# Modulation groups 9 to 14: the matmuls of two weight units issued as a pair, the later unit first

## The chip, the cores and the metric

The kernel runs on one core of a Trainium2 chip. PE is the matmul engine (its weight loads are shown apart as PEld), DVE the vector engine, ACT the scalar engine; SP issues nearly all transfers from HBM. The metric is the device time of one execution in microseconds. The kernel before took 1195.18 us, the median of 3 runs (1194.2 to 1197.44).

## The reference

One layer of a decoder trunk on 256 tokens of width 2048, all in float32:

```python
mod = jax.nn.silu(c) @ w_ada[l] + b_ada[l]          # 2048 -> 6 x 2048, one vector per sequence
shift_m, scale_m, gate_m, shift_f, scale_f, gate_f = jnp.split(mod[:, None, :], 6, axis=-1)
h = rms_norm(x, norm_mix_g[l]) * (1.0 + scale_m) + shift_m
proj = h @ w_in[l]                                   # q, k, v | xs, z, B, C, dt
...                                                  # attention on 8 heads; SSD (Mamba-2) on 16 heads
mix = jnp.concatenate([attn, ssm], axis=-1) @ w_out[l]
x = x + gate_m * mix
h = rms_norm(x, norm_ffn_g[l]) * (1.0 + scale_f) + shift_f
x = x + gate_f * conv_ffn(h, w_up[l], conv_ffn_w[l], conv_ffn_b[l], w_down[l])
```

`mod`, the modulation, is a product of one vector with a 2048 x 12288 matrix of 100 MB. `MOBA_BLOCK` is 256, the length of the sequence, so attention is plain causal attention with a bias.

## The kernel before, in words

Activations are kept transposed (features on partitions, 256 tokens along the row). Each weight matrix comes in units of 128 x 2048 float32 (1 MB). A gemm unit is split after landing: ACT casts it to a rounded high part (line 258), DVE subtracts to get the low part (line 259), and PE does three matmuls for each 128 x 128 block (lines 277 to 279), 48 for a unit.

The modulation's 96 columns of 128 are 24 groups of four, and each group comes as four units. For most groups DVE multiplies a unit with the broadcast vector and sums (line 210). For the groups in `ON_PE` (0, 6, 9 to 14 and 16) PE does it: unit i of a group holds a quarter of the rows for all four column blocks, and its four matmuls (line 217, tile `adp`, k = 0 to 3) each take a 128 x 32 stationary piece of the silu of c and stream 512 columns of the unit. Matmul k writes the partitions 32k to 32k+31 of one PSUM tile, so the four write different quarters of it, and the four units of a group add up there. After the last unit ACT copies the tile out (`row`, line 221) and four matmuls of one column turn it into columns (line 224, tile `adc`).

The order of the work is set in two steps. The table `ORDER` gives the program order up to the FFN: tokens such as `ada.9.0` (group 9, unit 0), V, Q, B, Z (input projection), S0 to S2 (attention of one head), T1 and T2 (SSD of two heads), O (output projection). Then a scheduler deals the instructions out to each engine's list by priority, which is the program order unless it is raised: the steps in `HPS`, attention and SSD among them, run under `tc.high_priority(offset=HP)`. Each engine works through its list in order; waits are semaphores. In the names of the lists, `wa` is the input projection's accumulator, `oa` the output projection's, `s`, `bp`, `pt`, `o` belong to attention, `xt` (line 533) is a transpose for SSD, `sg` and `y` (lines 577 and 578, four matmuls for two heads, on 64-column halves) are SSD's matmuls, `u1a` is the first FFN accumulator.

Weight units and modulation units share buffers: from the token `open` (before group 8) to `close2` (after group 14 has begun) there are three, `ws`; behind `close2` six. A buffer goes to the next transfer when its last reader is done, for a gemm unit DVE's second subtraction, for a modulation unit on PE its last matmul. SP issues the transfers in order and waits for that.

Of the kernel before, what the change touches and what calls it, by code (L numbers as in the profile page):

```python
# [30 lines left out]
HP = 200  # L31
# [63 lines left out]
def hymba_layer(ctx, tc, xT, c_row, cT, w_ada, vecs, consts, relb, onehot, w_vdt, w_in, w_out, w_up1, w_up, w_dn, outT):  # L95
    nc = tc.nc
    dve, act, pool, pe = nc.vector, nc.scalar, nc.gpsimd, nc.tensor
# [33 lines left out]
    def aux_tile(name):  # L131
        return psp.tile([P, 512], F32, tag="aux", name=name, bufs=7 - NACC)

    def tmp(name, n=T, tag="t256", bufs=4, dt=F32):
        return tp.tile([P, n], dt, tag=tag, name=name, bufs=bufs)
# [10 lines left out]
    c32 = cp.tile([P, KT, 32], F32, name="c32")  # L146
# [47 lines left out]
        return vec[:, CV[name] + i:CV[name] + i + n]  # L194


    ada_ps = {}

    def ada_load(g, i):
        ws = ws_tile(f"ada{g}_{i}")  # L200
        nc.sync.dma_start(ws[:, :D], w_ada[4 * g + i])
        return ws
# [3 lines left out]
    def ada_unit(g, i):  # L206
        ws = ada_pre.pop((g, i)) if (g, i) in ada_pre else ada_load(g, i)
        if g not in ON_PE:
            j = GROUPS[g][i]
            dve.scalar_tensor_tensor(ws[:, :D], ws[:, :D], 1.0, cb, op0=ALU.mult, op1=ALU.mult,  # L210
                                     accum_out=mod[:, j:j + 1])
            return
        if i == 0:
            ada_ps[g] = psp.tile([P, 512], F32, tag="ada", name=f"adp{g}", bufs=1)
        ps = ada_ps[g]
        for k in range(4):
            pe.matmul(ps[32 * k:32 * k + 32, :], c32[:, 4 * i + k, :], ws[:, k * 512:(k + 1) * 512],
                      start=i == 0, stop=i == 3)
        if i == 3:
            row = tmp(f"row{g}", 512, "row", 1)  # L220
            act.copy(row, ps)
            pc = aux_tile(f"adc{g}")
            for k in range(4):
                pe.matmul(pc[:, k:k + 1], row[:, k * P:(k + 1) * P], ones[:, 0:1], start=True, stop=True)
            t = GROUPS[g]
            if t[0] + 1 == t[1]:
                dve.tensor_copy(mod[:, t[0]:t[0] + 4], pc[:, 0:4])
            else:
                dve.tensor_copy(mod[:, t[0]:t[0] + 2], pc[:, 0:4:2])
                dve.tensor_copy(mod[:, t[1]:t[1] + 2], pc[:, 1:4:2])  # L230
# [9 lines left out]
    def ada_some(n, last=24):  # L240
        for _ in range(n):
            g, i = ada_next[0]
            if g < last:
                ada_unit(g, i)
                ada_next[0] = [g, i + 1] if i < 3 else [g + 1, 0]
# [19 lines left out]
    def weight_unit(src, n, name, hw=1024):  # L265
        ws = get_unit(src, n, name)
        parts = [hi_lo_part(ws, o, min(hw, n - o), name) for o in range(0, n, hw)]

        def block(i):
            wh, wl = parts[i * P // hw]  # L270
            j = i * P % hw
            return wh[:, j:j + P], wl[:, j:j + P]

        return parts, block
# [393 lines left out]
    def ada_step(g, i):  # L668
        ada_unit(g, i)
        if g < 8:  # L670
            if g in ON_PE:
                if i == 3:
                    ada_params(0, 2 * g, 2, "g_mix")
            elif i % 2:
                ada_params(0, 2 * g + i // 2, 1, "g_mix")
        else:
            ada_next[0] = [g, i + 1] if i < 3 else [g + 1, 0]
# [16 lines left out]
    for i in range(6):  # L694
        pe.matmul(ss1[:, 0:T], ones, (sqs[:, 1, i * T:i * T + T] if i < 4 else sqs[:, 0, (i - 4) * T:(i - 3) * T]),
                  start=i == 0, stop=i == 5)
# [27 lines left out]
    gp = mkpool("gT", NHALF + GX)  # L724
    h2 = fp.tile([P, KT, 512], F32R, name="h2")
    ada_unit(16, 0)
    rs2 = stats()

# [59 lines left out]
    for half in range(2):  # L788
        gts = []
        for jj in range(NHALF):  # L790
            j = half * NHALF + jj
            if half == 0:
                w = weight_unit(w_up1[NHALF + j], 2048, f"u2_{j}")
# [15 lines left out]
        for i in range(KT):  # L809
# [5 lines left out]
            for q in range(2):  # L815
                w = weight_unit(w_dn[half, i, q], 11 * P, f"d{half}_{i}_{q}")
# [106 lines left out]
```

## Time and profile before

| | |
|---|---|
| median of 3 runs | 1195.18 us (1194.2 to 1197.44) |
| profiled execution | 1199.98 us, span 1198.2 us |
| PE busy | 1166.6 us, 97% |
| DVE busy | 913.4 us, 76% |
| ACT busy | 636.7 us, 53% |
| granted clock, mean | 0.988 of 2.4 GHz |
| read from HBM | 305.98 MB, 257 GB/s over the span |

The profile is one execution. Busy time counts each engine's instructions; PE's are pipelined and overlap, so what one of them costs is better read from the distance between starts. A line of the profile is a line of the kernel before. The modulation groups 9 to 14 run between 243 and 424 us, and the FFN begins at 459 us.

### The profile page before, as it was taken

The numbers are of one execution on the slowest core, as the hardware profiler recorded it, in microseconds if no ns is written. First come the engines' busy times: TensorE is split into PE (matmuls) and PEld (weight loads), VectorE is DVE, ScalarE is ACT, GpSimd is POOL, SyncE is SP. The second block draws the span as 40 slices with busy tenths as digits, with TensorE's granted clock in tenths as the row PEclk, the third lists the DMA queues.
The fourth block names the chain that finished last, engine by engine and source line by source line (L and its number), as shares of the span: only waits on it lengthen the run. The fifth ranks groups of instructions, "written<-read, shape, count | busy, mean of one in ns | idle before, by whom it ended". The sixth has DMA issues, their size and how long they took to land.

```text
span 1198.2 us, 23400 instructions
## 1 busy us (share of the span) xinstructions
PE 1166.6 (97%) x9760; PEld 1115.8 (93%) x9760; DVE 913.4 (76%) x1371; ACT 636.7 (53%) x959; POOL 0.9 (0%) x7
## 2 busy tenths in 40 slices
PE   7899999999999999999999999999999999999996
PEld 4899999988888898999999999999999999999995
DVE  3899969977988898776599974446888889666554
ACT  4545434357786545445567654444555555555552
POOL 0000000000000000000000000000000000000000
PEclk8899999999999999999999999999999999999998
DMA  9989898777766996986565545557888776545552
GB/s 367 409 305 361 321 344 308 263 266 266 280 234 227 368 383 254 353 320 226 185 204 184 200 147 194 194 194 276 295 299 309 283 264 231 187 153 197 195 194 96
DMA packets 47443, 309.59 MB, mean 258 GB/s; under 512 B 5568, under 2 KB 6761, under 8 KB 16105
## 3 DMA queue, kind: packets, MB, share of 16 engines
q1 hardware_dynamic: 46170, 307.04, 70.2%
q10 hardware_dynamic: 1168, 1.06, 0.4%
q8 instruction: 76, 1.25, 0.4%
q14 instruction: 29, 0.24, 0.1%
HBM read 305.98 MB, written 2.11 MB: 257 GB/s over the span
## 4 chain that ended last, share of the span: by engine, by line
PE 85%; DVE 6%; DMA 5%; ACT 2%; issue 1%; SPq 0%; DVEq 0%; ACTq 0%
PE da L279 7%; PE da L278 7%; PE da L277 7%; PE ua L279 6%; PE ua L277 6%; PE ua L278 6%; PE wa L277 5%; PE wa L279 4%; PE wa L278 4%; PE va L348 4%; PE u2a L278 3%; PE u2a L277 3%; PE u2a L279 3%; PE oa L277 2%; PE oa L279 2%; PE oa L278 2%
## 5 line engine op out<-in xcount | busy, mean ns | idle before, releaser
L258 ACT CAST h_u<-s_u 128x1024 fp32r<-128x1024 f32 x176 | 183.4, 1050 | 187.0 <-PE ua L278 88.6
L259 DVE TENSOR_TENSOR l_u<-s_u,h_u 128x1024 fp32r<-128x1024 f32 x176 | 213.1, 1222 | 67.7 <-ACT h_u L258 67.3
L279 PE MATMUL ua<-h,l_u 128*128 128x256 f32 x704 | 194.4, 276 | 1.3 <-DVE l_u L259 1.3
L278 PE MATMUL ua<-h,h_u 128*128 128x256 f32 x704 | 194.3, 276 | 0.0
L277 PE MATMUL ua<-h,h_u 128*128 128x256 f32 x704 | 194.3, 276 | 0.0
L278 PE MATMUL da<-g,h_d 128*128 128x256 f32 x704 | 194.3, 276 | 0.0
L279 PE MATMUL da<-g,l_d 128*128 128x256 f32 x704 | 194.3, 276 | 0.0
L277 PE MATMUL da<-g,h_d 128*128 128x256 f32 x704 | 194.1, 276 | 0.0
L259 DVE TENSOR_TENSOR l_d<-s_d,h_d 128x1024 fp32r<-128x1024 f32 (+1 forms) x128 | 108.8, 887 | 83.6 <-ACT h_d L258 83.6
L277 PE MATMUL wa<-hT,h_w 128*128 128x256 f32 x576 | 163.9, 285 | 4.7 <-ACT h_w L258 3.7
L278 PE MATMUL wa<-hT,h_w 128*128 128x256 f32 x576 | 161.0, 280 | 0.0
L279 PE MATMUL wa<-hT,l_w 128*128 128x256 f32 x576 | 160.3, 281 | 0.2 <-DVE l_w L259 0.2
L258 ACT CAST h_d<-s_d 128x1024 fp32r<-128x1024 f32 (+1 forms) x128 | 98.2, 782 | 115.0 <-PE da L278 106.8
L210 DVE SCALAR_TENSOR_TENSOR ada<-ada,cb 128x2048 f32<-128x2048 f32 x60 | 136.9, 2285 | 16.1 <-DMA ada<-w_ada 16.0
L279 PEld LDWEIGHTS ua<-h,l_u 128*128 128x128 f32 x704 | 132.2, 188 | 1.5 <-DVE l_u L259 1.5
L278 PEld LDWEIGHTS da<-g,h_d 128*128 128x128 f32 x704 | 132.2, 188 | 0.0
L278 PEld LDWEIGHTS ua<-h,h_u 128*128 128x128 f32 x704 | 132.2, 188 | 0.0
L279 PEld LDWEIGHTS da<-g,l_d 128*128 128x128 f32 x704 | 132.2, 188 | 0.0
L277 PEld LDWEIGHTS ua<-h,h_u 128*128 128x128 f32 x704 | 132.2, 188 | 0.0
L277 PEld LDWEIGHTS da<-g,h_d 128*128 128x128 f32 x704 | 132.1, 188 | 0.0
L258 ACT CAST h_w<-s_w 128x1024 fp32r<-128x1024 f32 x72 | 73.7, 1048 | 90.4 <-PE wa L278 45.6
L277 PEld LDWEIGHTS wa<-hT,h_w 128*128 128x128 f32 x576 | 109.5, 190 | 13.0 <-ACT h_w L258 5.8
(237 smaller groups left out, 2681.9 us busy)
## 6 DMA issues: line engine op xcount, KB each, us to landing
ada<-w_ada SPq DMA_DIRECT2D x96, 1024.0 KB, 6.7
s_u<-w_up SPq DMA_DIRECT2D x88, 1024.0 KB, 4.9
s_d<-w_dn SPq DMA_DIRECT2D x64, 704.0 KB, 4.1
s_w<-w_in SPq DMA_DIRECT2D x36, 1024.0 KB, 6.9
s_o<-w_out SPq DMA_DIRECT2D x16, 1024.0 KB, 6.7
s_v<-w_vdt SPq DMA_DIRECT2D x8, 1040.0 KB, 7.9
x<-xT SPq DMA_DIRECT2D x4, 512.0 KB, 4.6
outT<-x SPq DMA_DIRECT2D x2, 640.0 KB, 3.0
```

What stands on the lines that cost most here:

```text
L210: dve.scalar_tensor_tensor(ws[:, :D], ws[:, :D], 1.0, cb, op0=ALU.mult, op1=ALU.mult, accum_out=mod[:, j:j + 1])
L258: act.copy(wh[:, :m], ws[:, o:o + m])
L259: dve.tensor_sub(wl[:, :m], ws[:, o:o + m], wh[:, :m].bitcast(F32))
L277: pe.matmul(o, whs, a[:, 0:T], start=first, stop=False)
L278: pe.matmul(o, whs, a[:, T:2 * T], start=False, stop=False)
L279: pe.matmul(o, wls, a[:, 0:T], start=False, stop=last)
L348: pe.matmul(va[tt][i][:, :n], lo if st == 1 else hi, (wl if st == 2 else wh)[:, s], start=f and st == 0, stop=l and st == 2)
```

## The change

For the groups 9 to 14 (`8 <= g < 16`; those of them that are on PE) the first of two units is only loaded and kept. When the second is there, its four matmuls are issued, at raised priority, and tied behind them the four of the first. The start flag of the group's accumulation moves to unit 1, the stop flag to unit 2. Groups 0, 6 and 16 go the old way.

```diff
-    ada_ps = {}
+    ada_ps, ada_held = {}, {}
...
         ps = ada_ps[g]
-        for k in range(4):
-            pe.matmul(ps[32 * k:32 * k + 32, :], c32[:, 4 * i + k, :], ws[:, k * 512:(k + 1) * 512],
-                      start=i == 0, stop=i == 3)
+
+        def products(n, w, first, last):
+            for k in range(4):
+                m = pe.matmul(ps[32 * k:32 * k + 32, :], c32[:, 4 * n + k, :], w[:, k * 512:(k + 1) * 512],
+                              start=first, stop=last)
+            return m
+
+        if 8 <= g < 16:
+            if i % 2 == 0:
+                ada_held[g] = ws
+                return
+            with tc.high_priority(offset=HP):
+                m = products(i, ws, i == 1, False)
+                with tc.issue_after(m.ins):
+                    products(i - 1, ada_held.pop(g), False, i == 3)
+        else:
+            products(i, ws, i == 0, i == 3)
         if i == 3:
```

The scheduler deals out a new order from there. PE's list is the same up to the 1662nd matmul, at 243 us, and again from a little behind the head of the FFN. SP's list differs in two places only (one unit of the output projection and one of group 16, each by a place or two). Lines of the changed kernel are 14 higher from line 218 on; the products are on its line 219.

PE's list in the middle of the input projection's last quarter, before: unit 3 of group 9 alone, between gemm matmuls and the second matmul stage of an attention head (`o`).

```order
L277 MATMUL wa_12_2840<-hT_142,h_w_2810 128x256
L278 MATMUL wa_12_2840<-hT_142,h_w_2810 128x256
L279 MATMUL wa_12_2840<-hT_142,l_w_2811 128x256
L217 MATMUL adp_2642<-ada_3_2899,c_98 32x512 x4
L467 MATMUL o_2888<-pts_2886,vdt 128x256
L468 MATMUL o_2888<-pts_2886,vdt 128x128
```

The same unit now, with unit 2 behind it, among the transposes (`pt`) of another head:

```order
L456 MATMUL s_2862<-qk_146 128x128
L219 MATMUL adp_2642<-ada_3_2895,c_98 32x512
L476 MATMUL pt_2878<-con,p_2730 128x128
L219 MATMUL adp_2642<-ada_3_2895,c_98 32x512
L477 MATMUL pt_2878<-con,p_2730 128x128
L219 MATMUL adp_2642<-ada_3_2895,c_98 32x512 x2
L219 MATMUL adp_2642<-ada_2_2798,c_98 32x512 x4
L292 MATMUL wa_12_2810<-hT_141,h_w_2802 128x256
```

Unit 3 has moved 36 matmuls forward, unit 2 32 matmuls back; the four matmuls of unit 3 stand in three pieces.

PE's list at the SSD output of the first two heads (`y`, T2.0), in the output projection's first half, before:

```order
L577 MATMUL y_3770<-L_3656,xdt 64x256
L578 MATMUL y_3770<-L_3656,xdt 64x128
L577 MATMUL y_3770<-L_3656,xdt 64x256
L578 MATMUL y_3770<-L_3656,xdt 64x128
L277 MATMUL oa_1_3852<-cat_3093,h_o_1_3848 128x256
L278 MATMUL oa_1_3852<-cat_3093,h_o_1_3848 128x256
L279 MATMUL oa_1_3852<-cat_3093,l_o_1_3849 128x256
L277 MATMUL oa_1_3852<-cat_3248,h_o_1_3848 128x256
L278 MATMUL oa_1_3852<-cat_3248,h_o_1_3848 128x256
L533 MATMUL xt_3776<-con,cxs 128x128 x2
```

And now:

```order
L293 MATMUL oa_1_3852<-cat_3024,l_o_1_3849 128x256
L591 MATMUL y_3766<-L_3652,xdt 64x256
L547 MATMUL xt_3772<-con,cxs 128x128
L592 MATMUL y_3766<-L_3652,xdt 64x128
L547 MATMUL xt_3772<-con,cxs 128x128
L591 MATMUL y_3766<-L_3652,xdt 64x256
L592 MATMUL y_3766<-L_3652,xdt 64x128
L571 MATMUL sg_2_3785<-am,tri_r 128x512
```

The four matmuls of `y`, in one piece before, stand in three pieces with a transpose in each gap.

## Rows read from the trace of the kernel before

**Rows 1.** The page: busy us (share of the span) and instructions of each engine.
```profile
PE 1166.6 (97%) x9760; PEld 1115.8 (93%) x9760; DVE 913.4 (76%) x1371; ACT 636.7 (53%) x959; POOL 0.9 (0%) x7
```

**Rows 2.** Busy time by stretch: from:to, us, engines' busy us, PEclk, DMA share, GB/s.
```profile
243.00:459.00 216.00, 213.38 (x1703) 179.91 (x1701) 179.42 (x365) 139.50 (x272) 0.00 (x0) 1.00 0.75 281
460.00:1198.00 738.00, 723.06 (x6340) 721.18 (x6338) 528.12 (x723) 390.30 (x555) 0.00 (x0) 0.99 0.64 226
```

**Rows 3.** Line 217 in 243 to 430 us: what ended its idle time.
```profile
  issue: 3.0, 10
```

**Rows 4.** PE in order of time: a lone product (start, us, instruction).
```profile
247.90 0.28 PE L279 MATMUL wa<-hT,l_w 128*128 128x256 f32 x1
248.10 1.05 PE L217 MATMUL adp<-ada,c 128*32 128x512 f32 x2
249.08 0.38 PE L277 MATMUL wa<-hT,h_w 128*128 128x256 f32 x1
249.30 0.28 PE L278 MATMUL wa<-hT,h_w 128*128 128x256 f32 x1
```

**Rows 5.** PE in order of time: eight products of two units, two records each.
```profile
375.55 0.28 PE L278 MATMUL oa<-cat,h_o 128*128 128x256 f32 x1
375.66 0.28 PE L279 MATMUL oa<-cat,l_o 128*128 128x256 f32 x1
375.87 1.92 PE L217 MATMUL adp<-ada,c 128*32 128x512 f32 x16
377.73 0.39 PE L277 MATMUL oa<-cat,h_o 128*128 128x256 f32 x1
377.95 0.28 PE L278 MATMUL oa<-cat,h_o 128*128 128x256 f32 x1
```

**Rows 6.** PE in order of time: y of two heads in one run; L578 and two transposes left out.
```profile
371.91 0.28 PE L277 MATMUL oa<-cat,h_o 128*128 128x256 f32 x1
372.12 0.66 PE L577 MATMUL y<-L,xdt 128*64 128x256 f32 x4
...
373.12 0.37 PE L278 MATMUL oa<-cat,h_o 128*128 128x256 f32 x1
```

**Rows 7.** PE in order of time: y in two halves around two transposes.
```profile
352.28 0.28 PE L279 MATMUL oa<-cat,l_o 128*128 128x256 f32 x1
352.49 0.65 PE L577 MATMUL y<-L,xdt 128*64 128x256 f32 x2
352.97 0.38 PE L578 MATMUL y<-L,xdt 128*64 128x128 f32 x2
353.28 0.44 PE L533 MATMUL xt<-con,cxs 128*128 128x128 f32 x2
353.65 0.65 PE L577 MATMUL y<-L,xdt 128*64 128x256 f32 x2
...
354.45 0.50 PE L557 MATMUL sg<-am,tri_r 128*128 128x512 f32 x1
```

**Rows 8.** PE groups by line, 243 to 459 us: busy, mean ns, idle before, releaser.
```profile
L277 PE MATMUL oa<-cats,h_o 128*128 128x256 f32 x128 | 35.9, 280 | 0.3 <-ACT h_o L258 0.3
L279 PE MATMUL oa<-cats,l_o 128*128 128x256 f32 x128 | 35.4, 278 | 1.1 <-DVE l_o L259 1.1
L533 PE MATMUL xt<-con,cxs 128*128 128x128 f32 x16 | 3.3, 286 | 0.4 <-ACT cxs L370 0.4
```

**Rows 9.** PE in order of time at the head of the FFN.
```profile
458.50 1.05 PE L224 MATMUL adc<-ones,row 128*128 128x1 f32 x8 [0.71 <-ACT row L221]
459.41 0.48 PE L277 MATMUL u1a<-h,h_u 128*128 128x256 f32 x2
```

**Rows 10.** SP's waits (us, times, longest) and landings of modulation units, 243 to 430 us.
```profile
SPq L201 <- PE adp L217: 52.8, 10, 10.3
SPq L252 <- PE adp L217: 34.7, 11, 10.1
...
DMA to landing us min/median/max: 4.9/6.8/9.3
```

## The prediction, made before the changed kernel ran

> **What bounds the kernel now.** I read the busy shares first, because they say which engine to count on: PE is busy for 97% of the span [rows 1]. Then the stretch in which the changed products stand, 243 to 459 us: 213.4 us of PE work in 216 us, at the full clock, with DVE at 83% and the DMA engines at 75% [rows 2]. So a PE instruction that is added there moves the end, and one that is saved moves it too, unless another wait is ready to take its place. Then the products' own line: in this stretch no wait of theirs is ended by a DMA, only "issue" before ten of them, 3.0 us [rows 3]. Waits for other things are few: 0.4 us at a transpose, 0.3 and 1.1 us at the first matmuls of the second output half [rows 8].
>
> The price of a product is read from start to start on PE, since durations overlap. Two neighbouring gemm matmuls are about 0.115 us apart (375.55 to 375.66 [rows 5]). A lone product: last gemm matmul at 247.90, product at 248.10, next gemm matmuls at 249.08 and 249.30 [rows 4]: 1.40 us from the matmul before to the second one behind, of which 0.23 would have passed anyway: 1.17 us for one product. Eight products of two units in one run: 375.66 to 377.95 [rows 5], 2.29 less 0.23, 2.06 us. Eight cost less than two lone ones, because the four products of a unit write four different 32-column groups and run beside each other; the fifth has to wait for the group of the first. So the unit of cost is a block: up to four products in a row with different groups. One block and one switch are 1.17, two blocks and one switch are 2.06: 0.89 us for a block, whether it holds one product or four, and 0.28 us for going into the narrow mode and out of it.
>
> **The change, part by part.** The loads, their sizes and the number of products stay. What changes is the order that the scheduler makes, from 243 us to the head of the FFN; behind that PE's list is the same to the end, and PE is busy there for 723 of 738 us [rows 2], so whatever is lost or won by 459 us arrives at the end.
>
> *Products of groups 9 to 14.* In the old order I count, group by group, 4, 4, 3, 4, 3, 3 runs, 21 in all, with 5, 5, 4, 4, 4, 4 blocks, 26. In the new order 8 of the 12 pairs stand as one run of eight. The other four are broken up, because other work of the same high priority comes between them: 6+2, 1+1+6, 1+7 and 1+7 products. That is 5, 3, 3, 2, 2, 2 runs, 17, with 7, 5, 5, 4, 4, 4 blocks, 29. Old: 26 x 0.89 + 21 x 0.28 = 29.0 us. New: 29 x 0.89 + 17 x 0.28 = 30.6 us. So four switches are saved, 1.1 us, and three blocks are added, 2.7 us: +1.55 us. Bounds: -1.1 us if the broken-off products hide beside their neighbours, +2.7 us if each of the four broken pairs pays one switch more where its pieces border on attention matmuls instead of gemm matmuls (4 x 0.28).
>
> *The SSD output matmuls (y).* They use 64-column halves, so they obey the same rule. Two heads' matmuls in one run with two transposes behind: 371.91 to 373.12, 1.21 us [rows 6]. The old order splits one pair of heads (y2) in two, with the transposes between: 352.28 to 354.45, 2.17 us [rows 7]. The new order keeps that split and breaks y0 and y1 into three pieces each, with a transpose in each gap. No row shows three pieces; I put them together from those of rows 7: in 0.21, L577 alone 0.48 and about 0.09 to leave (the 0.28 of a switch less 0.09 paid on the way in and 0.10 at the second matmul behind), a transpose 0.19 (two take 0.37), L578 alone 0.31, a transpose 0.19, the other half 0.80, together 2.27 us. Against 1.21 that is +1.06 for each, +2.1 us. Bounds: 0 if the pieces overlap with the transposes; +3.5 if each piece costs what a half does (352.28 to 353.28 less 0.12, 0.88; three make 2.64 where one run costs 0.90). I take 2.1, which is near the split that rows 7 show (+0.96 each).
>
> *Loads and buffers.* There are three weight buffers until the second half of the output projection, and the SP queue waits for products again and again: 52.8 + 34.7 us in 243 to 430 us [rows 10]. The earlier unit now holds its buffer until its partner is there, and SP issues in order, so behind it the next weight unit waits too, then ACT's and DVE's splitting of it, then the gemm. But the high priority also brings the later unit of every pair forward on PE, by 7 to 114 matmuls, and the earlier one ends sooner than before in 7 of the 12 pairs. Where the later product comes forward, the buffer goes sooner to the next load. I cost this at nothing: in the old order the products never waited for a load although SP waited for them. It costs something if PE gets to a pair before the later unit's load has landed, 4.9 us after its issue at best and 6.8 us in the middle [rows 10]; bounds 0 and +6 us (third rival).
>
> *Other waits.* The first transposes for SSD stand 54 matmuls earlier than before, and they already waited 0.4 us for ACT's SiLU [rows 8]; ACT's list now has that SiLU ahead of the other one, of the gate. From -0.45 to +2 us; I take 0. The 0.3 and 1.1 us at the second output half hang on a load issued behind the norm matmul; between that matmul and the waiting one stands the same amount of work in both orders: 0, bounds -1.4 and +1. At the FFN head the transposing matmuls of group 16, which waited 0.71 us for ACT and took 0.91 us until the first FFN matmul at 459.41 [rows 9], now stand behind the first eight of those. At best the 0.71 is saved; at worst the 0.91 is paid later in the stream. I take 0, since the first FFN matmul also waits for the normed input. Waits on DVE and ACT that a re-dealt order may bring have no row: the old order shows about 1.9 us of waits in this stretch, and I take as many for the new one, bounds -1.9 and +5.
>
> **Sum.** +1.55 + 2.1 = +3.7 us. The profiled execution took 1199.98 us, 1.8 of it outside its span, and would take 1203.7. It lies 4.8 us above the median of the runs shown, so I carry the difference over: 1195.18 + 3.7 = 1198.9 us, +0.31%. A change under 0.3%, 3.6 us here, can hardly be told from none, so this forecast lies on the line.
>
> **Rivals.**
> First: only switches count. Then the lone products and the pieces of y cost their 0.28 and hide otherwise. Entries into a narrow mode: 21 runs of products and 9 pieces of y before, 17 and 13 after, 30 both times: 1195.2 us. For it: the pieces stand among attention matmuls and transposes, and the scheduler took the spots for free. Against it: the lone product of rows 4 and the halves of rows 7 paid in full. The Trainium skill, "TensorEngine Tiling (Array Packing)", Key Properties, says that changing the tiling mode drains the engine while tiles of one mode work in parallel. By the drain alone the time would stay; the trace agrees that there is one, 0.28 us, but shows the block as the larger price.
>
> Second, not slower: the pairs pay. Four switches less (-1.1), the transposes' wait gone (-0.45), the 0.71 at the FFN head covered, and the pieces free: -2.3, 1192.9 us. It decides if every piece lies in time in which PE would have waited; with 2.6 us without work in 216 [rows 2] there is hardly room.
>
> Third: the later unit comes late. The price is a wait of PE at the first product of a pair, with all of PE queued behind it. If three of the twelve pairs come 1.9 us early (6.8 less 4.9, the load queued behind another), it is +5.7 on top: 1204.6 us. It decides from the point where the later load is issued less than 4.9 to 6.8 us ahead of the pair. For it: the later units move forward by up to 114 matmuls, 13 us, and the DMA engines are 75% busy. Against it: the buffers that these loads wait for mostly go free earlier too.
>
> **How the numbers follow.** Forecast 0.60, first rival 0.17, second 0.07, third 0.16. My forecast's own range is 1196.5 to 1201.5; a little more than half of it lies above the line of +0.3%, so 0.36 of its 0.60 is slower and 0.24 the same. The first rival is the same. Of the second, 0.04 is faster and 0.03 the same. The third is slower. Together: slower 0.52, the same 0.44, faster 0.04. The range from 1195.0 to 1204.5 leaves out the second rival, half of the third and about a third of the first, 0.2 in all.
>
> **What would show it.** On PE, the lone products of groups 9 to 11 should each take about 1.17 us from matmul to matmul, the unbroken pairs 2.06; y0 and y1 with their transposes some 2.3 us each; the FFN's first matmul should come 3 to 4.5 us later than 459.4. Busy PE in that stretch should stay near 99%. The forecast is wrong if lone products start beside their neighbours' matmuls, if a DMA ends waits at the first product of pairs, or if gaps on PE that DVE or ACT end add up to over 4 us.

## The result and the profile after

The changed kernel took 1203.18 us, the median of 6 runs (1200.45 to 1204.43), against 1196.31 us (1193.72 to 1198.67, 6 runs) of the kernel before beside it: ratio 1.0060, interval 1.0045 to 1.0074, so 5.4 to 8.9 us slower. A second measurement gave 1.0053 (1.0032 to 1.0074). The forecast said +3.7 us: the sign and half of the size. The time lies inside the stated range (1195.0 to 1204.5), but above the forecast's own (1196.5 to 1201.5).

The page of the changed kernel, its first part (as [rows 1]), and the two stretches of [rows 2]:

```profile
PE 1170.2 (97%) x9760; PEld 1116.3 (93%) x9760; DVE 912.5 (76%) x1371; ACT 638.4 (53%) x959; POOL 0.9 (0%) x7
```

```profile
243.00:459.00 216.00, 214.46 (x1677) 179.67 (x1679) 174.83 (x357) 139.21 (x269) 0.00 (x0) 1.00 0.72 275
460.00:1198.00 738.00, 726.40 (x6358) 723.92 (x6350) 530.87 (x731) 392.12 (x559) 0.00 (x0) 0.99 0.65 227
```

Up to 459 us PE is busy for 214.5 of 216 us and gets through 1677 matmul records where it got through 1703. That is the forecast's picture: hardly any new waits, but an order that is dearer on PE. The products' own line (as [rows 3]), and the three lines that wait (as [rows 8]):

```profile
  issue: 7.6, 25
```

```profile
L293 PE MATMUL oa<-cats,l_o 128*128 128x256 f32 x128 | 35.6, 278 | 0.8 <-DVE l_o L273 0.8
...
L547 PE MATMUL xt<-con,cxs 128*128 128x128 f32 x16 | 3.8, 297 | 0.6 <-ACT cxs L384 0.6
...
L571 PE MATMUL sg<-am,tri_r 128*128 128x512 f32 x8 | 3.6, 453 | 0.2 <-ACT L L579 0.2
```

No DMA ends a wait of a product. "Issue" before products rose from 3.0 us to 7.6, but a kernel below that beats both has 7.9 there: it belongs to the price of a run and is no loss by itself. SP waits for products about half as long as before, 45 us in place of 87, and never over 5.6 us at a time (as [rows 10]); it waits longer for DVE's subtraction in the output projection (`l_o`), 43 us in place of 21.

```profile
SPq L201 <- PE adp L219: 34.2, 14, 5.6
...
SPq L266 <- PE adp L219: 11.1, 9, 3.9
```

Then the head of the FFN, PE in order of time (as [rows 9]):

```profile
457.83 2.78 PE L219 MATMUL adp<-ada,c 128*32 128x512 f32 x24
461.32 0.51 PE L291 MATMUL u1a<-h,h_u 128*128 128x256 f32 x2 [0.70 <-ACT h L327]
462.36 0.39 PE L292 MATMUL u1a<-h,h_u 128*128 128x256 f32 x1 [0.54 <-DVE h L328]
...
463.18 1.31 PE L238 MATMUL adc<-ones,row 128*128 128x1 f32 x8
```

The granted clock there (from:to, us, PE, PEld, DVE, ACT, POOL busy, PEclk, DMA share, GB/s):

```profile
455.00:463.00 8.00, 6.76 (x49) 2.98 (x48) 6.77 (x12) 4.33 (x9) 0.00 (x0) 1.00 0.66 237
463.60:470.40 6.80, 6.80 (x33) 6.80 (x33) 5.40 (x12) 1.85 (x4) 0.00 (x0) 0.50 0.51 175
470.40:478.00 7.60, 7.60 (x69) 7.60 (x68) 5.20 (x5) 4.10 (x5) 0.00 (x0) 1.00 0.36 136
```

One wait of 0.71 us has become two, 0.70 and 0.54. The adc matmuls, which stood ahead of all FFN matmuls, follow behind the first eight, and from 463.6 to 470.4 us the clock stands at 0.5, 1.2 GHz: 33 records in 6.8 us, where the next 7.6 us hold 69. The kernel before has no such stretch there.

The two profiled executions differ by only 3.2 us (1203.19 and 1199.98), because that of before holds losses that the other lacks: a start that is 0.7 us longer, 3.4 us at 1.2 GHz behind 540 us and a wait of 1.3 us at 1000 us. So below the mix and the head are measured apart, between fixed places of the traces.

### The profile page after: what moved, and what is told of

It is laid out like the page before. It is cut to its first block, busy times and chain, and to the rows that moved or that the text cites. A ratio compares the mean times of both kernels' runs of the same rounds, so it can differ in the third digit from the quotient of the medians.

```text
span 1201.3 us, 23390 instructions
## 1 busy us (share of the span) xinstructions
PE 1170.2 (97%) x9760; PEld 1116.3 (93%) x9760; DVE 912.5 (76%) x1371; ACT 638.4 (53%) x959; POOL 0.9 (0%) x7
## 3 DMA queue, kind: packets, MB, share of 16 engines
q10 hardware_dynamic: 1168, 1.06, 0.4%
## 4 chain that ended last, share of the span: by engine, by line
PE 86%; DMA 5%; DVE 4%; ACT 2%; issue 2%; SPq 0%; DVEq 0%; ACTq 0%
PE ua L292 7%; PE da L293 7%; PE da L291 7%; PE ua L291 7%; PE ua L293 7%; PE da L292 7%; PE wa L291 5%; PE wa L292 5%; PE wa L293 5%; PE va L362 4%; PE u2a L291 3%; PE u2a L293 3%; PE u2a L292 3%; DMA s_u<-w_up 3%; PE adp L219 3%; PE oa L291 2%
```

## The experiments

Two distances are read in each trace. *Mix*: from the 1501st matmul record on PE to the last 24 product records, those of group 16 (before: 214.36 to 455.01, 240.65 us). *Head*: from there to the 100th record of `u1a` (before: 455.01 to 470.96, 15.95 us). The clock is the mean granted clock over all executions of a kernel. The mix of three executions whose order is that of before up to the head (before with the head moved, twice, and with the head far) differs from 240.65 us by 0.1 to 0.8 us: that is its scatter. Ratios are against the kernel before, timed beside each; measured microseconds below are worked out from them unless medians are named. Line numbers of the experiments differ by a few from those of the kernel that each is made from.

| kernel | time, us | ratio (interval) | mean clock | mix | head |
|---|---|---|---|---|---|
| before | 1195.7 to 1197.4 | 1 | 0.9911 | 240.65 | 15.95 |
| changed | 1203.18 | 1.0060 (1.0045 to 1.0074) | 0.9903 | +3.5 | +3.9 |
| changed again | 1202.77 | 1.0053 (1.0032 to 1.0074) | 0.9890 | +3.7 | +2.2 |
| changed, head back | 1199.04 | 1.0023 (1.0008 to 1.0039) | 0.9912 | +3.5 | 0.0 |
| before, head moved | 1198.52 | 1.0019 (1.0005 to 1.0033) | 0.9897 | +0.3 | +0.6 |
| the same again | 1198.25 | 1.0012 (0.9996 to 1.0028) | 0.9903 | +0.8 | +0.6 |
| before, head far | 1195.06 | 0.9999 (0.9982 to 1.0017) | 0.9912 | +0.1 | +0.8 |
| changed, head far | 1199.01 | 1.0024 (1.0009 to 1.0040) | 0.9913 | +4.1 | +0.8 |
| changed, y whole | 1198.57 | 1.0017 (1.0004 to 1.0030) | 0.9905 | -0.4 | +0.6 |
| pairs whole, head back | 1192.58 | 0.9980 (0.9963 to 0.9997) | 0.9906 | -3.3 | 0.0 |
| pairs and y whole, head back | 1191.22 | 0.9956 (0.9936 to 0.9975) | 0.9909 | -2.8 | 0.0 |
| changed, products interleaved | 1204.48 | 1.0083 (1.0056 to 1.0110) | 0.9900 | +8.6 | +0.6 |

### The changed kernel again

No edit.

> The changed kernel once more, as a control. Theory (head and clock): +6.9 us over before again, and in the profile the granted clock is 0.5 for some 7 us right behind the FFN's first matmuls (463 to 470 us), 3.4 us of the loss. Rival (the fall of the clock is an accident of one execution, as the one at 540 us in the profile of before may be): the profile shows it at another place or not at all, and then about 3.4 us less, +3.5 us over before.

Measured: +6.4 us by the medians; in the profile the clock falls at the same place, for half as long:

```profile
464.10:467.50 3.40, 3.40 (x18) 3.40 (x18) 3.40 (x10) 1.56 (x4) 0.00 (x0) 0.50 0.54 229
```

Head lengths line up with it: +0.6 us where the clock does not fall, +2.2 with 3.4 us at 1.2 GHz, +3.9 with 6.8 us. So two waits cost 0.6, and the fall half of its length. It stands in both profiled executions of this kernel, with a different length in each.

### The head put back

The operations that make the FFN's normed input (h2) are tied behind the row's copy (on ACT), the first FFN matmuls behind adc (on PE).

```diff
-    h2_last = h2_gen(0, 8)
+    with tc.issue_after(box["row"].ins):
+        h2_last = h2_gen(0, 8)
...
-            mm3(lead[j][:, 0:T], lead_hl[0][j][0][:, b], lead_hl[0][j][1][:, b], hk[i], i == 0, i == 7)
+            with tc.issue_after(box["adc"].ins):
+                mm3(lead[j][:, 0:T], lead_hl[0][j][0][:, b], lead_hl[0][j][1][:, b], hk[i], i == 0, i == 7)
```

> The changed kernel, with the FFN head as before: the copy of group 16's row stands ahead of the h2 operations on ACT, and the four adc matmuls ahead of the first u1a matmul on PE. The only edit on PE is that adc moves forward by 8 matmuls. Theory: the waits of 0.70 and 0.54 us and the stretch at 1.2 GHz go, the wait of 0.7 us for the row comes back: 1199.5 us, +3.3 us over before (the losses in the mix alone, +3.5). Rival 1 (the fall of the clock is an accident): the time stays within 0.6 us of the changed kernel's, +6.4 to +6.9. Rival 2 (the FFN head is worth nothing and the rest of the loss lies in the mix): +6.9.

Measured: +2.8 us (1.0 to 4.7), 3.7 us under the changed kernel's second measurement. The mean clock is back at 0.9912, and the head's rows are those of [rows 9] again:

```profile
460.15 1.05 PE L238 MATMUL adc<-ones,row 128*128 128x1 f32 x8 [0.71 <-ACT row L235]
461.06 0.48 PE L291 MATMUL u1a<-h,h_u 128*128 128x256 f32 x2
```

The mix keeps its +3.5. Rivals 1 and 2, which left the time where it was, fall.

### The head moved in the kernel before

`tail16` first issues the row's copy, then the adc matmuls; the diff shows the two places that call it. The second text is of a repetition.

```diff
+            if kt == 2:
+                with tc.issue_after(box["h"].ins):
+                    next(tail16)
...
+        if i == 1:
+            with tc.issue_after(m.ins):
+                list(tail16)
```

> The kernel before, with the FFN head of the changed kernel alone: ACT copies group 16's row behind three h2 operations, the adc matmuls stand behind the first 8 u1a matmuls. No product of groups 9 to 14 moves. Theory: two waits of together 1.2 us in place of one of 0.7, and the clock falls to 0.5 for some 7 us behind them: +3.5 to +4.0 us, 1200.1 us. Rival (the clock's fall is an accident or comes from the mix): +0.5 us at most, 1196.8 us.

> The kernel before with the changed kernel's FFN head alone (adc behind 8 matmuls) once more, on the same chip as the run with adc far behind. Theory B: mean granted clock about 0.9897 against 0.991 of before, +2.1 us over before, as the first time. Rival (the first time was chance): clock 0.991, +0.6 us or less.

Measured: +2.3 us (0.6 to 3.9) and +1.4 (-0.5 to 3.4), a clock of 0.9897 and 0.9903. In both profiled executions the two waits are there and the clock does not fall at the head (head +0.6). The head alone costs something between theory and rival: the waits, 0.6 us, and on average somewhat more. That the rest is a fall of the clock in part of the executions is inferred from the mean clock; no trace of this kernel shows one. The figure of +3.5 to +4.0 took the fall in one profiled execution for the usual one.

### The head with adc far behind

The same edit with `i == 7`, so that adc stands behind 44 FFN matmuls; then the same in the changed kernel.

> The kernel before with the FFN head moved, but with the four adc matmuls of group 16 behind 44 of the first FFN matmuls and not behind 8, so that the waits of 0.70 and 0.54 us stay and the narrow adc matmuls stand in the middle of gemm work. Theory A (the two waits alone make the clock fall in part of the executions): the mean granted clock stays near 0.9897 and the time near 1198.5 us. Theory B (it takes the waits and the adc matmuls together, close behind the narrow products): the mean clock returns to 0.991 and the time to about 1197.0 us, 0.6 us over before.

> The changed kernel, with the four adc matmuls of group 16 behind 44 of the first FFN matmuls in place of 8; nothing of the products or of y moves, the two waits at the head stay. Theory B (the clock falls where the waits and the narrow adc matmuls stand together): the mean granted clock returns from 0.9890 to 0.991 or more, the time to 1199.5 to 1200.5 us, +4 over before (3.5 of the mix and 0.6 of the waits), 2.5 us under the changed kernel. Theory A (the waits alone do it): the clock stays at 0.989 to 0.990, the time at 1202 us, +6 over before.

Both waits stay, the adc matmuls follow in the middle of gemm work (PE in order of time, kernel before with adc far):

```profile
458.25 0.50 PE L281 MATMUL u1a<-h,h_u 128*128 128x256 f32 x2 [0.70 <-ACT h L318]
459.29 0.39 PE L282 MATMUL u1a<-h,h_u 128*128 128x256 f32 x1 [0.54 <-DVE h L319]
...
464.35 0.95 PE L228 MATMUL adc<-ones,row 128*128 128x1 f32 x8
```

Measured: mean clock 0.9912 and 0.9913, time -0.1 us (-2.2 to 2.0) on before, +2.9 (1.1 to 4.8) in the changed kernel. By the mean clock theory B stands: the same two waits, without the narrow adc matmuls close behind, leave it up. The five measurements with adc behind eight FFN matmuls and the products in the changed or the old order (changed twice, before twice, y whole; 48 executions) have a mean clock of 0.9900; those of the same orders with the head back or adc far (36 executions) have 0.9912, the kernel before 0.9911 (81 executions). The two runs with whole pairs and the head back, further below, lie between, at 0.9906 and 0.9909; with them the second group is at 0.9910 (60 executions). A difference of 0.0012 of 1200 us is 1.4 us on average; the changed kernel alone, at 0.9897 over 12 executions, is 1.7 us behind the kernel before.

The mean clock doesn't say where the clock was low: the profiled executions spend 10.2 to 17.0 us at 1.2 GHz in their first 60 us alone. And the traces by themselves don't decide. Of the six with adc behind eight FFN matmuls only the two of the changed kernel show the fall at the head; neither of the two with adc far does. Elsewhere the clock fell behind waits with no one-column matmuls near. In the kernel before the clock falls behind 540 us, among FFN matmuls alone, behind waits of 0.27 and 1.45 us (the last row is of the granted clock):

```profile
538.03 0.39 PE L277 MATMUL u1a<-h,h_u 128*128 128x256 f32 x1 [0.27 <-ACT h_u L258]
539.99 0.38 PE L279 MATMUL u1a<-h,l_u 128*128 128x256 f32 x1 [1.45 <-DVE l_u L259]
...
540.50:543.90 3.40, 3.40 (x18) 3.40 (x18) 3.40 (x7) 2.40 (x4) 0.00 (x0) 0.50 0.64 186
```

In the changed kernel a wait of 1.45 us at the same place, at 546 us, is followed by no fall.

The Trainium skill, "TensorE: Matmul & The Clock Gate", A second HAM failure mode: psum-queue depth-cycling, says that short and frequent idle times of PE between groups of matmuls can make the clock swing. The trace agrees only in part: the waits ahead of the fall at the head are short, 0.70 and 0.54 us, but they are two and not many.

### y whole

```diff
-            with tc.high_priority(offset=HP):
+            with tc.high_priority(offset=HP * (3 if it[0] == "T2" else 1)):
```

> The changed kernel, with T2 at three times the raised priority: the four y matmuls of every pair of heads stand in one run (8 runs in place of 13 pieces). Runs and blocks of the products stay 17 and 29. Theory (a piece of y costs what the rows of before show): y0 and y1 give back 1.06 us each and y2 0.96, -3.1 us against the changed kernel: 1200.1 us, +3.8 over before; the clock still falls at the FFN head. Rival (the pieces hide beside the transposes, only narrow-mode entries count): 5 entries less at 0.28 us, -1.4 us: 1201.8 us.

Measured: +2.0 us (0.5 to 3.6), 4.2 under the changed kernel's second measurement; the mix loses all of its excess, from +3.6 to -0.4. (In this profiled execution the clock does not fall at the head.) PE in order of time at T2.0, changed kernel (as [rows 7]):

```profile
341.95 0.28 PE L293 MATMUL oa<-cat,l_o 128*128 128x256 f32 x1
342.16 0.65 PE L591 MATMUL y<-L,xdt 128*64 128x256 f32 x2
342.74 0.33 PE L547 MATMUL xt<-con,cxs 128*128 128x128 f32 x1
343.00 0.43 PE L592 MATMUL y<-L,xdt 128*64 128x128 f32 x2
343.36 0.33 PE L547 MATMUL xt<-con,cxs 128*128 128x128 f32 x1
343.62 0.65 PE L591 MATMUL y<-L,xdt 128*64 128x256 f32 x2
344.10 0.38 PE L592 MATMUL y<-L,xdt 128*64 128x128 f32 x2
344.42 0.51 PE L571 MATMUL sg<-am,tri_r 128*128 128x512 f32 x1
```

And with y whole (as [rows 6]):

```profile
341.65 0.28 PE L293 MATMUL oa<-cat,l_o 128*128 128x256 f32 x1
341.86 0.66 PE L591 MATMUL y<-L,xdt 128*64 128x256 f32 x4
342.34 0.39 PE L592 MATMUL y<-L,xdt 128*64 128x128 f32 x4
342.67 0.44 PE L547 MATMUL xt<-con,cxs 128*128 128x128 f32 x2
342.86 0.48 PE L571 MATMUL sg<-am,tri_r 128*128 128x512 f32 x1
```

The same work takes 2.47 us in pieces and 1.21 whole: +1.26, and y1 shows the same. With 0.96 for y2 that is 3.5 of the 4.0 us that the mix gives back. The rival's 1.4 us in all falls.

### Whole pairs, and everything together

The first run has products at `10 * HP` and the head back; the second adds the edit of y.

> As the run with three edits, but T2 at its usual raised priority: y stands in 14 pieces, y0 and y1 in three pieces each, y2 in three. Products 12 runs, 24 blocks. Theory: products -4.3, y0 and y1 +1.28 each (measured with y whole), y2 +0.3, waits -0.5: -2.0 us against before, 1194.4 us, 3.7 us more than with y whole. Rival (pieces of y hide beside transposes): within 1.5 us of the run with y whole.

> The changed kernel with all three edits: products at ten times the raised priority, so that all 12 pairs stand in one run (12 runs, 24 blocks), T2 at three times (y in 8 whole runs), and the FFN head as before. Theory (block 0.89, switch 0.28, y): products 24 x 0.89 + 12 x 0.28 = 24.7 us against 29.0 before, -4.3; y2 whole, -1.0; the waits at the second output half 0.7 less; no added fall of the clock: -5 to -6 us, 1190.4 to 1191.4 us. Rival 1 (only switches count): 9 runs of products and 1 of y less, 10 x 0.28, -2.8 us: 1193.6 us. Rival 2 (whole pairs make other work or loads late): no gain, 1196.4 us or more.

Measured: -2.4 us (-4.4 to -0.4) and -5.3 us (-7.6 to -3.0) by the ratios. Both beat the kernel before, the second with an interval that takes in the theory's -5 to -6 and just leaves out rival 1's -2.8. Between the two the medians differ by 1.4 us where 3.7 was expected. By its time, within 1.5 us, the rival of the first run (the pieces of y hide) is met; the rows are against it, since y0, y1 and y2 take 2.46 us each in the first run and 1.21 in the second, 3.75 us in all. In the profiled executions the mix even has the sign the other way, -3.3 and -2.8, because the second caught waits between 243 and 300 us that the first did not:

```profile
PE wa L293 <- DVE l_w L273: 0.8, 1, 0.8
PE wa L291 <- ACT h_w L272: 0.7, 1, 0.7
PE pt L475 <- DVE p L459: 0.5, 1, 0.5
PE pt L475 <- ACT sqa L487: 0.4, 1, 0.4
```

They lie ahead of all y matmuls, where PE's order is the same in both runs. Whether every execution of the second run has them, its one trace can't say. One run of products, at 300.25 us, waited for its load as well, its first weight load 0.79 us and its first matmul 0.59 (line 219 of the second, 243 to 430 us):

```profile
  issue: 7.9, 26
  DMA ada<-w_ada: 1.4, 2
```

So the mechanism of the prediction's third rival exists, in an order that brings pairs further forward. It did not act in the changed kernel, where no DMA ends a wait of a product.

### Products interleaved

```diff
-                m = products(i, ws, i == 1, False)
-                with tc.issue_after(m.ins):
-                    products(i - 1, ada_held.pop(g), False, i == 3)
+                w, m = ada_held.pop(g), None
+                for k in range(4):
+                    for n, u, f, l in ((i, ws, i == 1, False), (i - 1, w, False, i == 3)):
+                        with (tc.issue_after(m.ins) if m else ExitStack()):
+                            m = pe.matmul(ps[32 * k:32 * k + 32, :], c32[:, 4 * n + k, :],
+                                          u[:, k * 512:(k + 1) * 512], start=f, stop=l)
```

> The changed kernel, with the eight products of a pair in turn, unit by unit, for each 32-column group: neighbours write the same group, so that 61 blocks stand in 15 runs in place of 29 in 17. Number, size and loads of the products are the same. Theory (a block costs 0.89 us, whether it holds one product or four): 32 blocks more, 2 runs less: +27.9 us on the changed kernel, about 1231 us. Rival 1 (the cost is streaming, eight products of a pair cost the same in any order; only switches count): -0.6 us, 1202.5 us. Rival 2 (only two neighbours of one group wait for each other, and the next group starts beside them: 5 steps for 8 products in place of 2): about half, +14 us or so more likely to be seen in the distance of the products' starts.

Measured: +9.9 us (6.7 to 13.1, 4 executions), some 3 over the changed kernel, not 28: the theory falls, and rival 2 with it. Eight interleaved products in one run cost what eight cost in unit order:

```profile
373.79 0.28 PE L294 MATMUL oa<-cat,h_o 128*128 128x256 f32 x1
374.00 1.95 PE L232 MATMUL adp<-ada,c 128*32 128x512 f32 x16
375.87 0.39 PE L295 MATMUL oa<-cat,h_o 128*128 128x256 f32 x1
376.10 0.28 PE L296 MATMUL oa<-cat,l_o 128*128 128x256 f32 x1
```

373.79 to 376.10 is 2.31 us, less 0.23 it is 2.08. But two products of the same group take as long as eight of four groups, while two of different groups take as long as one. First this kernel (two of one group), then the changed kernel (two of two groups), at the same place of the program:

```profile
251.70 1.90 PE L232 MATMUL adp<-ada,c 128*32 128x512 f32 x4
253.54 0.38 PE L294 MATMUL wa<-hT,h_w 128*128 128x256 f32 x1
```

```profile
250.66 1.05 PE L219 MATMUL adp<-ada,c 128*32 128x512 f32 x4
251.64 0.39 PE L291 MATMUL wa<-hT,h_w 128*128 128x256 f32 x1
```

1.84 us from the first start to the next gemm matmul against 0.98. So a block is real, but neighbours do not decide it. These rows fit groups that each work off their own products beside the others: a run costs 0.28 us plus 0.89 for every product of the group that has most of them in it. By that count this order has 29 blocks in 15 runs, as many blocks as the changed kernel. Rival 1's time is nearest, for another reason. The mix is 5.1 us longer than in the changed kernel: 1.7 of it is half of a stretch of 3.4 us at 1.2 GHz at 331 us (behind two waits, of 0.73 and 1.68 us), and 3.1 are more waits for DVE and ACT (4.7 us in place of 1.6). The Trainium skill, "TensorEngine Tiling (Array Packing)", Key Properties, says that tiles of one mode operate independently; these rows agree, down to the order in which their instructions stand.

## Why the prediction was right, and where it was wrong

*Products.* Forecast +1.55. On the way to 332 us, where groups 9 to 11 are done, the block count alone makes 11 runs and 17 blocks against 11 and 14, +2.7; the traces show about +2.6 there (+3.0 by equal records, less 0.3 for one more unit done and 0.14 for the transposes' longer wait). Lone products cost 1.21 to 1.27 us between attention matmuls and transposes, unbroken pairs 2.05 to 2.06 everywhere, against 1.17 and 2.06. The size stands, and whole pairs give it back: the mix with 12 whole runs is 3.3 us shorter than before although y is still broken (1.2 of it are fewer waits). That the fifth product of a run waits for the group of the first also stands. Too narrow was the block as "up to four products in a row with different groups": the interleaved run shows that a group's share of the run counts, in any order. The changed order has 29 blocks by either count, so this did not touch the forecast.

*y.* Forecast +1.06 for each of two, measured +1.26: +2.5 in place of +2.1.

*Waits and loads.* Taken as nothing. The transposes wait 0.14 us more and `sg` 0.19, the second output half 0.7 less. No load came late. With products by the count (+2.7 for groups 9 to 11, -1.1 for four runs fewer in groups 12 to 14) and y these sum to +3.7; three traces of this order show +3.5, +3.7 and +3.5, and the one with adc far +4.1. The forecast had +3.7: up to the FFN head its sum was right, and each term to within 0.7 us.

*The FFN head.* This is the step that failed. The forecast took it as 0, "since the first FFN matmul also waits for the normed input", between -0.71 and +0.91. The reason was half seen. In the old order the row's copy and the adc matmuls filled the very time in which the normed input came; moved behind, they leave it empty, and PE waits 0.70 and 0.54 us for that input: +0.6. And the bounds were made of waits alone. The clock, which fell behind those waits and the adc matmuls in both traces of the changed kernel, was in no term: by the mean clock +1.7 us on average over its 12 executions, and 3.3 in the profiled one. In the old head, too, adc stands right behind a wait, of 0.71 us, and in four traces the clock stays up there; so one wait with adc behind it is not enough.

*The sum.* +3.6 in the mix, +0.6 and +1.7 at the head make +5.9 us, inside both intervals of the time (5.4 to 8.9 and 3.8 to 8.9). The remaining 0.5 to 1.3 us can't be told from the scatter of the runs. Why the clock falls in some executions and not in others, and for how long, stays open.

*The range.* That the time lies inside the stated range is in part luck. Its upper part was there for the third rival, loads that come late (1204.6 us), and that did not happen; a loss that the forecast had in no term took the room.

*Rivals and signs.* "Only switches count" fell with y whole, "the pairs pay" with the mix of the four traces of this order, and "the later unit comes late" because no DMA ends a wait of a product in the changed kernel. PE stayed busy for 99% of the stretch, and its waits there for DVE and ACT were 1.6 us, far under the 4 that were named as a sign of being wrong. The sign that the FFN's first matmul would come 3 to 4.5 us later failed in form: it came 1.9 us later (461.32 against 459.41), because adc no longer stood ahead of it and this execution's start was 0.7 us shorter; the products of group 16 ahead of it came 2.8 later.

## What to carry to other kernels

In this kernel matmuls on narrow column groups are best counted by run: one price for entering the mode (0.28 us), and one for each product of the fullest group (0.89 us for 512 columns in float32), whatever the order; a scheduler that slips a transpose into such a run makes it pay again. Raising a piece of work in priority shifts what other engines do far behind it: look at the next place where PE waits, and at what filled that wait before. The price of short waits in a row need not be their length, since the clock can fall behind them: two waits of together 1.24 us, with one-column matmuls close behind, were followed by 3.4 and 6.8 us at 1.2 GHz. One profiled execution can't tell how often that happens; set it against the mean clock of many. Of the orders tried, whole pairs, whole y and the old head was the fastest, at 1191.22 us, 0.9956 of the kernel before (0.9936 to 0.9975).

## What was unexpected of the hardware

- The granted clock fell to 1.2 GHz for 6.8 and 3.4 us behind two waits of 0.70 and 0.54 us with eight one-column records close by, in both profiled executions of the changed kernel, and in none of the four of other kernels with the same head; with those records 44 matmuls later the mean clock over 24 executions was 0.9913, against 0.9911 in the kernel before and 0.9900 over 48 executions with them close.
- Two products of one 32-column group took 1.84 us from start to the next gemm matmul, two of different groups 0.98, and eight of four groups 1.86 in unit order and 1.87 interleaved.
- Four 64-column matmuls of two heads with two transposes took 1.21 us as one run, 2.17 in two pieces and 2.47 in three.
